# Two of a pair's four weight sums, from VectorE to a plain and an accumulating transfer

## The chip, the cores and the metric

The kernel runs on one core of a Trainium2 chip. The metric is the device time of one execution in microseconds (us). Of the kernel before, three timed runs and one profiled execution are given.

## The reference

A decoder layer on 512 tokens of width 1024, float32: a SwiGLU feed-forward, a mixer (dilated attention beside a gated linear recurrence), and a second SwiGLU feed-forward, each inside norms and a residual sum. The change lies in the two feed-forwards:

```
f = (silu(x @ w_gate) * (x @ w_up)) @ w_down      # 1024 -> 2816 -> 1024
h = h + 0.5 * rms_norm(f, norm_post)
```

## The kernel before, in words

**Number format.** A float32 product is made of three reduced ones. `split` (L301 to L303) makes a high part on ScalarE (L302) and a low part on VectorE (L303, the number less its high part); `mm3` and `seventh` multiply high by high, high by low and low by high.

**Feed-forward.** The 2816 hidden columns are 22 blocks of 128. The first 6 blocks (first feed-forward) or 3 (second) are multiplied plainly ("std"). Every later block f is a **pair**: its gate block g and its up block u, each 1024 x 128, are multiplied together by a Strassen-like scheme with 7 products in place of 8, with g and u as the two block columns. The rows of each are cut in two halves of 512 (g0, g1, u0, u1 in the tile: 4 row chunks of 128 columns side by side, so 128 x 512). The seven weight operands are g0, g1, u1 and four sums: u0+u1, u0+u1+g0, u0+g0 and u0+u1+g0+g1.

**`w_forms` (L684 to L702)** makes a pair's operands. It loads two raw tiles of 128 x 1024 (ur = u0 u1, gr = g0 g1) on the SP queue (L242; pool of 4 raw tiles), makes the four sums on VectorE (L691: u0+u1, L692: that + g0, L693: u0+g0, L696: the second + g1), and splits four tiles: a (g0, g1), b (the tile s12 with two sums), c (ur, one sum and u1) and d (the last sum). a, b and c are wide weight tiles (tag w8, 4 buffers), d is a narrow one (w4, 2 buffers). s12 has the tag s with 2 buffers. Products are named p1 to p7: a holds p1 and p2, b p6 and p5, c p7 and p4, d p3.

**`seven_on` (L733 to L760)** multiplies a pair from block 5 on in the order p1, p5, p6, p2, p7, p3, p4, 12 matmuls of 256 columns each (L729 to L731). The activation operand of p6 is the tile tx; the others' are tiles called big. ScalarE moves sums between PSUM tiles (L743), VectorE adds two results (L950, L955), and the result goes through `into` (L960 and L913 to L928) to become the operand of the down-projection.

**Down-projection.** It is made by seven products too, over groups of four blocks, in steps (`down7`, L1034 to L1052) that lie between the pairs of the next group: 12 or 24 matmuls of 512 columns (L1043 to L1045) and their weights by `d_forms` (L970 to L1002), which takes raw tiles and w8 tiles from the same pools.

**Order.** `ffn_order` (L66 to L90) writes the order of events: `prep` of pair f+1 (its `w_forms`) stands before `prod` of pair f. All of a pair's weight work is traced with a priority of 100 instructions ahead (AHEAD), moves out of PSUM with 200 (EVAC). A planner at compile time orders each engine's queue by these priorities and places the tiles; each engine then runs its queue strictly in order and waits for semaphores. Loads on SP follow one stream in device memory (`stream_plan`), in the order of their use, so a pair's two raw blocks lie one after the other there. The POOL queue issues transfers only: copies of activations (L655), the kept residual (L536, L1721, L1151) and gain rows (L449).

**The mixer** uses `w_forms` as well (through `pair_of`, L1340), for 16 pairs.

Of the kernel before, what the change touches and what calls it, by code (L numbers as in the profile page):

```python
# [10 lines left out]
F32 = mybir.dt.float32  # L11
F32R = mybir.dt.float32r
AF = mybir.ActivationFunctionType
ALU = mybir.AluOpType
AX = mybir.AxisListType

P = 128
T = 512
D = 1024
KC = D // P  # L20
NF = 22
FF_PARTS = ((0, 4), (4, 8), (8, 12), (12, 16), (16, 22))
NSTD = {1: 6, 2: 3}

SEVEN = range(4)
STEPS_AT = {1: ((6, 7, 7, 8), range(9, 13), range(13, 17), range(17, 21)),
# [5 lines left out]
RAW_W = 1024  # L32
# [3 lines left out]
AHEAD = 100  # L36
# [29 lines left out]
def ffn_order(n):  # L66

    order = [("std", f) for f in range(NSTD[n])]  # L70
    after = {}
    for a in SEVEN:
        for i, f in enumerate(STEPS_AT[n][a]):
            after.setdefault(f, []).append((a, i))
    ready = False
    for f in range(NSTD[n], NF):
        if not ready:
            order.append(("prep", f))
        steps = after.get(f, [])
        order += [("prepd",) + s for s in steps]  # L80
        ready = f + 1 < NF
        if ready:
            order.append(("prep", f + 1))
        order += [("seeds",) + s for s in steps[:1]]
        order.append(("prod", f))
        for m, s in enumerate(steps):
            if m:
                order.append(("seeds",) + s)
            order.append(("down7",) + s)
    return order  # L90
# [70 lines left out]
def stream_groups():  # L161

    groups, cur, w = [], [], 0
    for key, width in stream_plan():
        if w + width > RAW_W or (cur and cur[0][0][0] == "start"):
            groups.append(cur)
            cur, w = [], 0
        cur.append((key, w, width))
        w += width
    groups.append(cur)  # L170
    return groups
# [12 lines left out]
def hybrid_layer(ctx: ExitStack, tc: tile.TileContext, xT: bass.AP, xN: bass.AP, wst: bass.AP,  # L184
                 first: bass.AP, rows: bass.AP, consts: bass.AP, bias: bass.AP, out: bass.AP):
    nc = tc.nc
    DVE, ACT, PE = nc.vector, nc.scalar, nc.tensor
# [3 lines left out]
    wpool = ctx.enter_context(tc.tile_pool(name="wpool", bufs=4))  # L191
# [39 lines left out]
    groups = stream_groups()  # L231
    state = {"g": 0, "i": 0, "off": 0, "raw": None, "ahead": AHEAD, "split": None}
# [21 lines left out]
    def raw_two(key, dst=None):  # L254

        return [raw_of(key + (n,), None if dst is None else dst[:, i * RAW_W:(i + 1) * RAW_W])
                for i, n in enumerate(("lo", "hi"))]

    def fetch(key, slot=None, ahead=0):

        with tc.high_priority(offset=ahead if slot else state["ahead"]):
            src = raw_of(key)
            w = src.shape[-1]
            t = slot() if slot else w8() if w > 512 else w4()
            split(t[:, 0, :w], t[:, 1, :w], src)
            return t[:, 0, :w], t[:, 1, :w]

    def w8():
        return wpool.tile([P, 2, 1024], F32R, name="w8", tag="w8", bufs=4)

    def w4():
        return wpool.tile([P, 2, 512], F32R, name="w4", tag="w4", bufs=2)
# [28 lines left out]
    def split(dh, dl, src):  # L301
        state["split"] = ACT.activation(dh, src, AF.Copy).ins  # L302
        state["low"] = DVE.tensor_sub(dl, src, dh.bitcast(F32)).ins  # L303

    def acc_ps():
        return psum.tile([P, T], F32, name="acc", tag="acc", bufs=5)
# [23 lines left out]
    def gemm(ps, wt, x, sl=slice(0, T), ks=None):  # L330
        n = x.n
        a, b = k128(wt[0], n), k128(wt[1], n)
        for k in ks or range(n):
            mm3(ps, a[:, k, :], b[:, k, :], x.hi[k][:, sl], x.lo[k][:, sl], k == 0, k == n - 1)
# [346 lines left out]

    spool = [None]

    def w_forms(key):  # L684

        with tc.high_priority(offset=AHEAD):
            ur, gr = raw_two(key)
            u0, u1, g0, g1 = (r[:, i * 512:(i + 1) * 512] for r in (ur, gr) for i in range(2))
            s12 = spool[0].tile([P, 2, 512], F32, name="s12", tag="s", bufs=2)
            s1, s2 = s12[:, 0, :], s12[:, 1, :]  # L690
            DVE.tensor_add(s2, u0, u1)  # L691
            DVE.tensor_add(s1, s2, g0)  # L692
            DVE.tensor_add(u0, u0, g0)  # L693
            a, b, c, d = w8(), w8(), w8(), w4()
            split(a[:, 0, :], a[:, 1, :], gr)
            DVE.tensor_add(g1, s1, g1)  # L696
            split(b[:, 0, :], b[:, 1, :], s12.rearrange("p s c -> p (s c)"))
            split(c[:, 0, :], c[:, 1, :], ur)
            split(d[:, 0, :], d[:, 1, :], g1)
            lo, hi = slice(0, 512), slice(512, 1024)  # L700
            return {"p1": a[:, :, lo], "p2": a[:, :, hi], "p6": b[:, :, lo], "p5": b[:, :, hi],
                    "p7": c[:, :, lo], "p4": c[:, :, hi], "p3": d}  # L702
# [156 lines left out]
    def ffn(n, x, r, forms_x, apool, pss):  # L859
# [70 lines left out]
        def std_out(psg, psu, f):  # L930

            g = tmp("g")
            if r is None:
                ACT.activation(g, psg, AF.Silu)
                into(f, lambda dst, v: DVE.tensor_mul(dst, v(psu), v(g)))
                return
            u = tmp("u0")
            DVE.tensor_mul(g, psg, r)
            ACT.activation(g, g, AF.Silu)
            DVE.tensor_mul(u, psu, r)  # L940
            into(f, lambda dst, v: DVE.tensor_mul(dst, v(u), v(g)))
# [28 lines left out]
        def d_forms(a, i):  # L970

            x, w = sevens[a], {}

            def form(name, src):
                w[name] = w8()
                split(w[name][:, 0, :], w[name][:, 1, :], src)

            with tc.high_priority(offset=AHEAD):
                raw = [raw_of(("dq", n, a, q)) for q in SEVEN_RAW[i]]
                if i == 0:  # L980
                    x["sum"] = apool.tile([P, 2, D], F32, name="sum", tag="wd", bufs=1)[:, 0, :]
                sd = x["sum"]
                if i == 0:
                    g0, u0 = raw
                    form("p1", g0)
                    DVE.tensor_add(sd, g0, u0)
                    form("p7", sd)
                elif i == 1:
                    u1, = raw
                    form("p4", u1)  # L990
                    DVE.tensor_add(sd, sd, u1)
                    form("p6", sd)
                elif i == 2:
                    u0, u1 = raw
                    DVE.tensor_add(u0, u0, u1)
                    form("p5", u0)
                else:
                    g1, = raw
                    form("p2", g1)
                    DVE.tensor_add(sd, sd, g1)  # L1000
                    form("p3", sd)
            return w  # L1002
# [63 lines left out]

        keys = [(w, n, i) for i in range(NSTD[n]) for w in ("gate", "up")]
        forms = {}
        for ev in ffn_order(n):
            if ev[0] == "std":  # L1070
                j = ev[1]
                while len(pss) < 2 * j + 2:
                    pss.append(acc_ps())
                    gemm(pss[-1], fetch(keys[len(pss) - 1]), x)
                with tc.high_priority(offset=EVAC if j == NSTD[n] - 1 else 0):
                    std_out(pss[2 * j], pss[2 * j + 1], j)

                for step in steps[j:] if j == min(NSTD[n], 4) - 1 else steps[j:j + 1]:
                    step()
            elif ev[0] == "prep":  # L1080
                forms[ev[1]] = w_forms(("gu", n, ev[1]))
            elif ev[0] == "prepd":
                forms[ev[1:]] = d_forms(*ev[1:])
            elif ev[0] == "seeds":
                for g in groups(ev[2])[:3]:
                    seed(ev[1], *g)
            elif ev[0] == "down7":
                down7(*ev[1:], forms.pop(ev[1:]))
            else:
                prod(ev[1], forms.pop(ev[1]))  # L1090
        a = len(FF_PARTS) - 1
# [32 lines left out]
    for k in range(KC):  # L1124
        wh, wl, raw = wts[k]
# [77 lines left out]
    with ExitStack() as mx:  # L1203
# [126 lines left out]
        order = [("pair",) + p for ps in pairs for p in ps] + [("pair", 52 + c, 53 + c) for c in range(0, KC, 2)]  # L1330
        forms = {}
# [8 lines left out]
        def pair_of(key):  # L1340

            i = order.index(key)
            if i + 1 < len(order):
                forms[order[i + 1]] = w_forms(order[i + 1])
            return forms.pop(key)

        def qk(hd):
# [147 lines left out]
        for c in range(0, KC, 2):  # L1495
            g, u = tmp("g"), tmp("u")
            seven_wide(t, pair_of(("pair", 52 + c, 53 + c)), [g[:, h] for h in HALVES], [u[:, h] for h in HALVES],
                       then=gate)
# [10 lines left out]
    with ExitStack() as mx:  # L1509
# [183 lines left out]
        for c in range(KC):  # L1693
            if c < 3:
                ps = pss[c]
            else:
# [17 lines left out]
                 {(1, 3): lambda: (bd2.turn(0), bd2.turn(1))})  # L1714
    keys = [(w, 2, i) for i in range(NSTD[2]) for w in ("gate", "up")]
    pss = gemm_first(keys[:NFIRST], u2, [spare(ap2)["tx"]],
# [5 lines left out]
    grow5, _ = gains(ap2, 4)  # L1722
# [138 lines left out]
```

## Time and profile before

| | |
|---|---|
| Three timed runs | 1209.67, 1210.02, 1210.19 us |
| Profiled execution | 1209.61 us, of which the span of the instructions is 1207.8 |
| First feed-forward's pairs | about 60 to 310 us |
| Second feed-forward's pairs | about 880 to 1168 us |
| Bytes moved | 149.77 MB, 124 GB/s over the span |
| SP queue's share of the 16 DMA engines | 32.9% |
| POOL queue's share of the 16 DMA engines | 4.3% |

How to read it: engines are PE (TensorE matmul), PEld (its weight loads), DVE (VectorE), ACT (ScalarE), POOL (GpSimd) and SP (SyncE, which only issues transfers). In a row of groups stand line, engine, operation, written tile <- read tiles, shapes, count, then busy us in all, mean ns of one, and the idle time of the engine just before, with what ended most of it. In a row of the timeline stand start and duration in us, then what runs, and in brackets idle time before it and what ended it. A row of DMA issues gives count, size of one, and the median time from issue to landing. Ends of matmuls are modelled and overlap the next one's start, so the pace of matmuls is read from their starts.

### The profile page before, as it was taken

What the parts mean: (1) busy time and instruction counts of PE and PEld (TensorE: products, weight loads), DVE (VectorE), ACT (ScalarE), POOL (GpSimd) and SP (SyncE); (2) the same over time, 40 slices, a digit from 0 to 9 for tenths busy, and PEclk for the clock granted to TensorE, in tenths of its full rate; (3) what the DMA queues carried; (4) which work ended last, traced back from release to release, by engine and by line L of the source; (5) the groups of instructions that cost most, each with busy time, mean ns of one, the idle gap of its engine ahead of it and who ended that gap; (6) DMA issues with size and microseconds to landing.
All of it is one profiled execution on the core that took longest, in us unless ns stands there. A gap on an engine that the chain in (4) does not pass through costs nothing.

```text
span 1207.8 us, 18850 instructions
## 1 busy us (share of the span) xinstructions
PE 1198.6 (99%) x7222; PEld 1070.1 (89%) x7222; DVE 1033.3 (86%) x1626; ACT 831.8 (69%) x1447; POOL 26.1 (2%) x51
## 2 busy tenths in 40 slices
PE   9999999999999999999999999999999999999997
PEld 8889999999888888888888888888899999999996
DVE  7999888989689899999868999774799888889964
ACT  6566787887566576777736988734566687778763
POOL 0000000000011000000000000000100000000000
PEclk9999999999999999999999999999999999999999
DMA  7224343434725232222323532235443333333441
GB/s 267 88 92 139 120 139 109 137 117 150 250 106 154 71 101 91 89 87 80 122 67 110 176 121 88 88 107 189 140 142 121 121 125 117 128 120 126 125 173 70
DMA packets 45819, 149.77 MB, mean 124 GB/s; under 512 B 5152, under 2 KB 8608, under 8 KB 45728
## 3 DMA queue, kind: packets, MB, share of 16 engines
q1 hardware_dynamic: 38160, 131.09, 32.9%
q0 software_dynamic: 7280, 17.30, 4.3%
q8 instruction: 56, 0.92, 0.3%
q14 instruction: 35, 0.29, 0.1%
q10 hardware_dynamic: 288, 0.17, 0.0%
HBM read 138.06 MB, written 6.29 MB: 120 GB/s over the span
## 4 chain that ended last, share of the span: by engine, by line
PE 92%; DVE 4%; DMA 2%; ACT 1%; issue 1%; DVEq 0%; ACTq 0%
PE acc L779 10%; PE acc L729 9%; PE acc L731 9%; PE acc L730 9%; PE acc L315 7%; PE acc L317 7%; PE acc L316 7%; PE acc L780 5%; PE aux L1043 4%; PE aux L1044 4%; PE aux L1045 4%; PE acc L433 2%; PE acc L432 2%; PE acc L431 2%; DVE w L303 2%; DMA raw<-in_w 2%
## 5 line engine op out<-in xcount | busy, mean ns | idle before, releaser
L303 DVE TENSOR_TENSOR w<-raw,w 128x1024 fp32r<-128x1024 f32 (+1 forms) x272 | 296.9, 1097 | 32.2 <-ACT w L302 31.4
L302 ACT ACTIVATE w<-raw 128x1024 fp32r<-128x1024 f32 (+1 forms) x272 | 259.5, 958 | 90.0 <-PE acc L317 48.2
L729 PE MATMUL acc<-big,w 128*128 128x256 f32 x860 | 243.6, 283 | 0.0
L731 PE MATMUL acc<-big,w 128*128 128x256 f32 x860 | 243.4, 283 | 0.0
L730 PE MATMUL acc<-big,w 128*128 128x256 f32 x860 | 243.3, 283 | 0.0
L729 PEld LDWEIGHTS acc<-big,w 128*128 128x128 f32 x860 | 164.8, 192 | 1.8
L730 PEld LDWEIGHTS acc<-big,w 128*128 128x128 f32 x860 | 164.8, 192 | 1.5
L731 PEld LDWEIGHTS acc<-big,w 128*128 128x128 f32 x860 | 164.8, 192 | 0.0
L779 PE MATMUL acc<-big,w 128*128 128x512 f32 x380 | 136.5, 398 | 0.0
L780 PE MATMUL acc<-big,w 128*128 128x256 f32 x380 | 107.5, 283 | 0.0
L1043 PE MATMUL aux<-w,xf 128*128 128x512 f32 x224 | 87.3, 392 | 0.6 <-ACT w L302 0.6
L1044 PE MATMUL aux<-w,xf 128*128 128x512 f32 x224 | 87.5, 391 | 0.0
L1045 PE MATMUL aux<-w,xf 128*128 128x512 f32 x224 | 87.2, 389 | 0.0
L779 PEld LDWEIGHTS acc<-big,w 128*128 128x128 f32 x380 | 71.4, 188 | 16.0 <-ACT acc L784 0.2
L780 PEld LDWEIGHTS acc<-big,w 128*128 128x128 f32 x380 | 71.7, 189 | 0.3
L303 DVE TENSOR_TENSOR w<-s,w 128x1024 fp32r<-128x1024 f32 x51 | 62.2, 1220 | 3.2 <-ACT w L302 2.7
L315 PE MATMUL acc<-xf,w 128*128 128x512 f32 (+1 forms) x168 | 59.2, 354 | 0.0
L316 PE MATMUL acc<-xf,w 128*128 128x512 f32 (+1 forms) x168 | 58.7, 350 | 0.0
L317 PE MATMUL acc<-xf,w 128*128 128x512 f32 (+1 forms) x168 | 58.5, 349 | 0.0
L302 ACT ACTIVATE w<-s 128x1024 fp32r<-128x1024 f32 x51 | 53.9, 1057 | 6.2 <-PE acc L731 3.0
L779 PE MATMUL acc<-rb,w 128*128 128x512 f32 x152 | 55.5, 397 | 0.0
L743 ACT ACTIVATE c<-acc 128x256 f32<-128x256 f32 x68 | 25.8, 383 | 35.3 <-PE acc L731 35.3
(458 smaller groups left out, 2919.5 us busy)
## 6 DMA issues: line engine op xcount, KB each, us to landing
raw<-in_w SPq DMA_DIRECT2D x232, 512.0 KB, 3.5
big<-xf POOLq DMA_DIRECT2D x6, 512.0 KB, 3.3
gains<-in_rows POOLq DMA_DIRECT2D x5, 512.0 KB, 5.4
h<-in_x SPq DMA_DIRECT2D x8, 256.0 KB, 5.1
h<-in_xn POOLq DMA_DIRECT2D x4, 512.0 KB, 6.7
kept_m<-h POOLq DMA_DIRECT2D x4, 512.0 KB, 2.9
vals<-in_w SPq DMA_DIRECT2D x4, 512.0 KB, 6.0
h<-kept_m POOLq DMA_DIRECT2D x4, 512.0 KB, 6.2
```

Source lines behind the costliest of these rows:

```text
L302: state["split"] = ACT.activation(dh, src, AF.Copy).ins
L303: state["low"] = DVE.tensor_sub(dl, src, dh.bitcast(F32)).ins
L315: PE.matmul(ps, wh, xh, start=first, stop=False)
L316: PE.matmul(ps, wh, xl, start=False, stop=False)
L317: PE.matmul(ps, wl, xh, start=False, stop=last)
L729: PE.matmul(ps, wh, xh, start=start and k == 0, stop=False, skip_group_check=True)
L730: PE.matmul(ps, wh, xl, start=False, stop=False, skip_group_check=True)
L731: PE.matmul(ps, wl, xh, start=False, stop=k == 3, skip_group_check=True)
L779: PE.matmul(part, wh, at(BOTH, k), start=start and k == 0, stop=False, skip_group_check=True)
L780: PE.matmul(cross, wl, at(0, k), start=False, stop=k == 3, skip_group_check=True)
L1043: PE.matmul(ps, xh, wh, start=first and j == 0, stop=False, skip_group_check=True)
L1044: PE.matmul(ps, xh, wl, start=False, stop=False, skip_group_check=True)
```

## The change

For the pairs from block 8 on in the first feed-forward and from block 5 on in the second, two sums are made by transfers that POOL issues. `sums_ahead` takes a tile s, fills both halves with u0 by a plain transfer, and adds u1 to the first half and g0 to the second by an accumulating transfer, which waits until the plain one has landed. It is traced right after the operands of the pair before have been made, that is ahead of the `prod` of the pair two before. `w_forms_summed` then loads g0 and g1 (one transfer) and u1 (a transfer of half the size) on SP, and makes the other two sums on VectorE: u0+u1+g0 into the empty half of ur, and that + g1 into the second half of gr. Splits are a (g0, g1: p1, p2), b (s: p5, p7), c (ur: p6, p4) and d (p3). In the mixer nothing changes: 16 pairs never reach the index 99.

```
@@ -21,6 +21,7 @@
 NF = 22
 FF_PARTS = ((0, 4), (4, 8), (8, 12), (12, 16), (16, 22))
 NSTD = {1: 6, 2: 3}
+SUMMED = {1: 8, 2: 5}
 
 SEVEN = range(4)
 STEPS_AT = {1: ((6, 7, 7, 8), range(9, 13), range(13, 17), range(17, 21)),
@@ -681,7 +682,56 @@
 
     spool = [None]
 
-    def w_forms(key):
+    starts, summed, end = {}, {}, 0
+    for grp in groups[1:]:
+        starts[grp[0][0]] = end
+        end += (grp[-1][1] + grp[-1][2]) * P
+
+    def rows_of(key, o, *dims):
+        return bass.AP(tensor=wst.tensor, offset=wst.offset + starts[key + ("lo",)] + o,
+                       ap=[[RAW_W, P], *dims, [1, T]])
+
+    def sums_ahead(key):
+
+        with tc.high_priority(offset=AHEAD):
+            s = spool[0].tile([P, 2, T], F32, name="s12", tag="s", bufs=2)
+            nc.gpsimd.dma_start(s, rows_of(key, 0, [0, 2]))
+            nc.gpsimd.dma_start(s, rows_of(key, T, [P * RAW_W - T, 2]), accum_op=ALU.add)
+            summed[key] = s
+
+    def w_forms_summed(key):
+
+        s = summed.pop(key)
+        with tc.high_priority(offset=AHEAD):
+            g = state["g"]
+            assert state["i"] == 0 and [k for k, _, _ in groups[g] + groups[g + 1]] == [key + ("lo",), key + ("hi",)]
+            assert state["off"] == starts[key + ("lo",)]
+            gr, ur = (wpool.tile([P, RAW_W], F32, name="raw", tag="raw", bufs=4) for _ in range(2))
+            nc.sync.dma_start(gr, rows_of(key, P * RAW_W, [T, 2]))
+            nc.sync.dma_start(ur[:, T:], rows_of(key, T))
+            state["g"], state["off"] = g + 2, state["off"] + 2 * P * RAW_W
+            a, b, c, d = w8(), w8(), w8(), w4()
+            split(a[:, 0, :], a[:, 1, :], gr)
+            DVE.tensor_add(ur[:, :T], s[:, 0, :], gr[:, :T])
+            split(b[:, 0, :], b[:, 1, :], s.rearrange("p s c -> p (s c)"))
+            split(c[:, 0, :], c[:, 1, :], ur)
+            DVE.tensor_add(gr[:, T:], ur[:, :T], gr[:, T:])
+            split(d[:, 0, :], d[:, 1, :], gr[:, T:])
+            lo, hi = slice(0, T), slice(T, D)
+            return {"p1": a[:, :, lo], "p2": a[:, :, hi], "p5": b[:, :, lo], "p7": b[:, :, hi],
+                    "p6": c[:, :, lo], "p4": c[:, :, hi], "p3": d}
+
+    def w_forms(key, then=None):
+
+        if key in summed:
+            w = w_forms_summed(key)
+        else:
+            w = w_forms_made(key)
+        if then:
+            sums_ahead(then)
+        return w
+
+    def w_forms_made(key):
 
         with tc.high_priority(offset=AHEAD):
             ur, gr = raw_two(key)
@@ -1078,7 +1128,8 @@
                 for step in steps[j:] if j == min(NSTD[n], 4) - 1 else steps[j:j + 1]:
                     step()
             elif ev[0] == "prep":
-                forms[ev[1]] = w_forms(("gu", n, ev[1]))
+                f = ev[1]
+                forms[f] = w_forms(("gu", n, f), ("gu", n, f + 1) if SUMMED[n] <= f + 1 < NF else None)
             elif ev[0] == "prepd":
                 forms[ev[1:]] = d_forms(*ev[1:])
             elif ev[0] == "seeds":
@@ -1341,7 +1392,7 @@
 
             i = order.index(key)
             if i + 1 < len(order):
-                forms[order[i + 1]] = w_forms(order[i + 1])
+                forms[order[i + 1]] = w_forms(order[i + 1], order[i + 2] if 99 <= i + 2 < len(order) else None)
             return forms.pop(key)
 
         def qk(hd):
```

## The prediction

> **What bounds the kernel now.** I read the page's busy line first, then the table by stretches, then what TensorE waits for, and last the timeline around one of those waits.
>
> ```profile
> span 1207.8 us, 18850 instructions
> PE 1198.6 (99%) x7222; PEld 1070.1 (89%) x7222; DVE 1033.3 (86%) x1626; ACT 831.8 (69%) x1447; POOL 26.1 (2%) x51
> ```
>
> TensorE (PE) is busy for all but 9.2 us of the span. VectorE (DVE), which the change relieves, has 86%. The execution took 1209.61 us, 1.8 beyond its span, and the median of the three timed runs is 1210.02, so one execution stands within 0.4 us of it.
>
> ```profile
> 240.00:260.00 20.00, 20.00 (x145) 18.92 (x145) 18.35 (x23) 17.34 (x31) 0.00 (x0) 1.00 0.33 105
> 300.00:320.00 20.00, 20.00 (x129) 18.27 (x128) 13.64 (x18) 11.79 (x20) 2.09 (x4) 1.00 0.85 304
> 1000.00:1020.00 20.00, 19.80 (x153) 19.02 (x152) 14.88 (x20) 14.56 (x26) 0.00 (x0) 1.00 0.42 142
> 1020.00:1040.00 20.00, 20.00 (x143) 18.80 (x142) 19.97 (x28) 16.37 (x28) 0.00 (x0) 1.00 0.31 106
> ```
>
> Columns after the stretch: its length, busy us of PE, PEld, DVE, ACT and POOL, the granted clock, the DMA share, GB/s. In the first feed-forward PE has no idle time. In the second it loses 0.20 us in a stretch where DVE has 5 us to spare, and none in the next, where DVE is busy for 19.97 of 20. So a full DVE doesn't by itself stop PE. At 300 to 320 the DMA engines are busy for 0.85 of the time and PE still works for 20.00.
>
> ```profile
> PE aux L1043 <- ACT w L302: 0.6, 3, 0.2
> PE aux L1378 <- DVE qk L792: 0.7, 1, 0.7
> PE acc L729 <- ACT acc L743: 0.4, 1, 0.4
> ...
> 1013.28 1.05 ACT L302 ACTIVATE w<-raw 128x1024 fp32r<-128x1024 f32 x1
> 1013.90 0.28 PE L731 MATMUL acc<-big,w 128*128 128x256 f32 x1
> 1014.39 0.73 PE L1043 MATMUL aux<-w,xf 128*128 128x512 f32 x2 [0.20 <-ACT w L302]
> ```
>
> Only the first wait lies in the stages that change (the other two come at the attention and before the recurrence). Matmuls overlap, so the loss is read from starts: 256-column products start 0.12 us apart, here 0.49 passed, 0.37 is lost. Three times that is **1.1 us, about all that PE can get back in the feed-forwards**. What ends it is the high part of a down-projection weight on ACT, not a sum on DVE.
>
> **The change, part by part.** Pairs 8 to 21 of the first feed-forward (14) and 5 to 21 of the second (17) change: 31.
>
> *Removed.*
>
> ```profile
> L692 DVE TENSOR_TENSOR s<-s,raw 128x512 f32<-128x512 f32 x51 | 34.9, 685 | 12.3 <-DMA raw<-in_w 12.1
> L691 DVE TENSOR_TENSOR s<-raw 128x512 f32<-128x512 f32 x51 | 34.9, 684 | 6.1 <-DMA raw<-in_w 6.0
> L693 DVE TENSOR_TENSOR raw<-raw 128x512 f32<-128x512 f32 x51 | 34.8, 682 | 0.0
> ```
>
> The transfers make u0+u1 (L691) and u0+g0 (L693). The sums of L692 and L696 stay on DVE. That is 31 x (0.684 + 0.682) = 42 us of DVE's 1033. DVE's waits for raw weights in front of the sums (up to 18 us over 51 pairs) shrink too. All of it lies beside PE, which lost 1.1 us there. Value: 0; ends: 0 and -1.1.
>
> *Added: two transfers from POOL for each pair.*
>
> ```profile
> raw<-in_w SPq DMA_DIRECT2D x232, 512.0 KB, 3.5
> big<-xf POOLq DMA_DIRECT2D x6, 512.0 KB, 3.3
> h<-in_xn POOLq DMA_DIRECT2D x4, 512.0 KB, 6.7
> ...
> 860.46 0.76 POOL L655 DMA_DIRECT2D big<-xf  x1 [6.27 <-ACT xf L553]
> ```
>
> The plain one moves u0 twice (512 KB), the accumulating one 512 KB of u1 and g0. Issue: 0.76 us on POOL each. Landing of the plain one: 3.3, at most 6.7. No row shows an accumulating transfer: at the low end it costs a plain one, 3.3; at the high end it makes three passes (source, old sum, new sum) at the slowest row, 20.1; I take two passes at the nearest row of that size, 6.6. It can't gain anything. The chain plain, landing, accumulate, landing is 0.76 + 3.3 + 0.76 + 6.6 = **11.4 us**, between 8.1 and 28.3.
>
> What covers it:
>
> ```profile
> 1100.75 1.22 DVE L303 TENSOR_TENSOR w<-s,w 128x1024 fp32r<-128x1024 f32 x1
> 1127.89 1.22 DVE L303 TENSOR_TENSOR w<-s,w 128x1024 fp32r<-128x1024 f32 x1
> 1154.67 1.22 DVE L303 TENSOR_TENSOR w<-s,w 128x1024 fp32r<-128x1024 f32 x1 [0.53 <-ACT w L302]
> ...
> 292.18 1.19 POOL L449 DMA_DIRECT2D gains<-in_rows  x2 [291.73 <-DVE w L303]
> 1140.58 0.54 POOL L449 DMA_DIRECT2D gains<-in_rows  x1 [257.70 <-DVE w L303]
> ```
>
> The sum tile has two buffers, so a pair's transfer can begin when the split of the pair two before it has read its sums. The three rows are such splits, each two pairs after the other, where pairs follow fastest: from the end of one, 1101.97, to the high part on ACT ahead of the next (1.06 us before 1127.89) are 24.9 us; the second interval gives 24.5. So 11.4 fits with 13 to spare; only the upper end, 28.3, doesn't. POOL does nothing before 292 us in the first feed-forward and between 882.88 and 1140.58 in the second: nothing is queued ahead of the new transfers. The gains behind them wait for the last down-projection sum anyway. If the cover were gone, what is queued behind the waiting sum on DVE is the low part of the next split and then the PSUM sums L955, L950 and L960, for which the next products wait. Value: 0.
>
> *Loads on SP.* The pair's gate block comes first (512 KB) and of the up block only its second half (256 KB), still on two of the four raw buffers. Bytes moved go from 1.0 to 1.75 MB a pair, 24 MB more in all. No PE time goes with a higher DMA share as such (300 to 320, above), but a load beside POOL's traffic lands later:
>
> ```profile
> raw<-in_w SPq DMA_DIRECT2D x12, 512.0 KB, 4.7
> ```
>
> This is the same load in the stretch 290 to 330, with six 512 KB transfers of POOL: 4.7 instead of 3.5, **1.2 us later**. The Trainium skill, "DMA: Bandwidth & Descriptors", section "Issuing engines are not separate DMA queues", speaks against the change: transfers from any engine end on the same 16 DMA engines and interleave, so a second issuer brings no bandwidth. The trace agrees, by those 1.2 us; by that rule the rival below grows, and my sum stays.
>
> *Moved: which weights share a buffer.* Split b now holds p5 and p7 (was p6 and p5), c holds p6 and p4 (was p7 and p4). Products run p1, p5, p6, p2, p7, p3, p4, 12 matmuls x 0.12 = 1.44 us each. The four wide weight buffers are handed on as products end:
>
> ```profile
> 1003.96 0.28 PE L731 MATMUL acc<-tx,w 128*128 128x256 f32 x1
> 1004.56 1.05 ACT L302 ACTIVATE w<-raw 128x1024 fp32r<-128x1024 f32 x1
> 1005.40 0.28 PE L731 MATMUL acc<-big,w 128*128 128x256 f32 x1
> 1005.72 1.06 ACT L302 ACTIVATE w<-s 128x1024 fp32r<-128x1024 f32 x1
> 1009.72 0.28 PE L731 MATMUL acc<-big,w 128*128 128x256 f32 x1
> 1010.50 1.04 ACT L302 ACTIVATE w<-raw 128x1024 fp32r<-128x1024 f32 x1
> ...
> 1027.84 1.22 DVE L303 TENSOR_TENSOR w<-raw,w 128x1024 fp32r<-128x1024 f32 x1
> 1031.47 0.28 PE L729 MATMUL acc<-tx,w 128*128 128x256 f32 x1
> 1059.85 1.22 DVE L303 TENSOR_TENSOR w<-raw,w 128x1024 fp32r<-128x1024 f32 x1
> 1062.73 0.28 PE L729 MATMUL acc<-tx,w 128*128 128x256 f32 x1
> ```
>
> p6 alone reads the tile tx, which dates the products. The next pair's a follows the end of p6, b the end of p2, c the end of p4: ACT makes them as buffers come free. With b held until p7, a and b come 1.44 us later each; c as before. But c is now needed at p6, not 2 x 1.44 = 2.88 us later at p7. Its low part ends at 1029.06 and at 1061.07, p6 starts at 1031.47 and 1062.73: **2.4 and 1.66 us remain** where 5.3 and 4.5 were. Value: 0, as long as c isn't more than 1.66 us later than today.
>
> The sum: 1209.61 + 0 + 0 + 0 = 1209.6 against the profiled execution; against the median of the runs, **1210.0**. Most of the 42 us of DVE time turns into DVE's idle time.
>
> **Rivals.**
>
> *Late c (slower).* Place: the c split, read by p6. a and b come 1.44 us later into the stretch where DVE also makes the PSUM sums; if DVE hands all of it on and the up half lands 1.2 us later, c is 2.64 late: 0.24 over the margin of 2.4, 0.98 over that of 1.66. A mean of 0.6 on half of the 31 pairs is 9 us, 1219; on all of them 19 us, 1229. It decides from 1.66 us on. For: the loads lengthen, and the margin shrinks by 2.88 in every pair. Against: DVE gets 1.37 us back per pair, about what the move takes.
>
> *Late sums (slower).* The accumulating transfer is near its upper end, 28.3 against 24.5: 3.8 us of waiting in the about 8 pairs that follow fastest, 30 us, 1240. Then the sums aren't ahead of their use at all, and the change doesn't do what it says. Against: 13 us of slack at my value.
>
> *Faster.* PE gets back the 1.1 us of its waits in the feed-forwards, and the planner, whose order of every queue is made anew, happens also to lose those of the mixer (0.7 and 0.4 in the list): about 1207.3. The first alone, 1208.9, can't be told from no change. Against: the 1.1 us end on ACT and on a buffer that PE frees.
>
> **How the numbers follow.** About 0.2% (2.4 us) is what a measurement of this kernel tells from no change. Forecast, within 1208.3 to 1212.4: 0.62. Late c: 0.26. Late sums: 0.06. Faster: 0.06. So faster 0.06, same 0.62, slower 0.32. The range runs from 1208.3, which leaves out the faster case, to 1218, which takes in the forecast and the lighter half of late c; what is left out is some 0.2. The forecast's own range is 1208.3 to 1212.4.
>
> **What the profile of the changed kernel would show.** The four groups of sums of pairs fall from 51 to 20 instructions each, two new ones of 31 appear, DVE's busy time falls by about 42 us, PE's matmul count stays, and PE's idle time stays near 9 us. The accumulating transfer's landing should be 3.3 to 20.1, nearest 6.6, and no engine should wait for long on the sum tile. Late c shows as PE waits in front of products on tx, ended by ACT or DVE w of lines 302 and 303; late sums as DVE or ACT waits ended by a DMA into s. I am wrong if PE's waits in the feed-forwards grow to more than 2.4 us, or if a wait that I read as a buffer's was DVE's and PE gains more than 2.4.

## The result, and the profile after

The changed kernel takes 1252.59 us (median of 4 runs, 1248.14 to 1255.90) against 1210.11 of the kernel before in the same comparison (4 runs, 1209.67 to 1210.26): ratio **1.035, 95% interval 1.0315 to 1.0384, slower**. The profiled execution took 1253.95 us, 1.75 beyond its span. The prediction said 1210.0 with a range to 1218.0: it was wrong, by 42.6 us. Against the kernel before of the same comparison the change loses 42.5 us.

The page of the kernel after, its span and its busy line:

```profile
span 1252.2 us, 18905 instructions
PE 1216.0 (97%) x7222; PEld 1080.3 (86%) x7222; DVE 998.3 (80%) x1564; ACT 833.9 (67%) x1447; POOL 86.8 (7%) x113
```

DVE's busy time fell by 35.0 us (1033.3 before), where the prediction had 42, mostly because it added up the durations of 62 sums, while on DVE the end of one overlaps the start of the next (L692 of 0.69 us and L693 start 0.60 apart, at 1001.07 and 1001.67 of before). PE now has 36.2 us without work in the span (9.2 before), and for the same 7222 matmuls it is busy 17.4 us longer. These are two separate losses: PE waits, and PE at times runs slower. Most of the waits have one shape. The kernel after, its waits (engine, tile and line, what ended the wait: us in all, times, longest):

```profile
PE aux L1093 <- ACT aux L1082: 15.3, 7, 3.1
PE acc L779 <- ACT c L886: 4.5, 1, 4.5
PE aux L1093 <- ACT facc L1098: 3.6, 2, 2.3
...
DVE raw L1045 <- DMA raw<-in_w: 45.8, 8, 7.8
DVE raw L715 <- DMA s<-in_w: 12.7, 2, 6.7
```

L1093 is the first product of a down-projection step (L1043 before), L1082 the ScalarE copy that seeds its PSUM tile. Neither is touched by the change. L1045 is the sum of the step i = 2, `DVE.tensor_add(u0, u0, u1)` (L995 before). DVE waits 45.8 us there for a raw weight, at 8 places, the 4 groups of both feed-forwards. In the kernel before, the same operation waited 0.9 us over two places:

```profile
DVE raw L995 <- DMA raw<-in_w: 0.9, 2, 0.6
```

**One such place, step by step.** The kernel after, the timeline from 1069 to 1091 us: POOL's transfers, SP's loads, then DVE, ACT and PE.

```profile
1069.99 0.75 POOL L698 DMA_DIRECT2D s<-in_w  x1 [9.28 <-DVE w L304]
1075.14 1.20 POOL L699 DMA_DIRECT2D s<-in_w  x1 [4.40 <-DMA s<-in_w]
1073.26 2.68 SPq L243 DMA_DIRECT2D raw<-in_w  x2
1074.36 1.23 DVE L304 TENSOR_TENSOR w<-raw,w 128x1024 fp32r<-128x1024 f32 x1 [0.52 <-ACT w L303]
1083.04 1.22 DVE L1045 TENSOR_TENSOR raw<-raw 128x1024 f32<-128x1024 f32 x1 [7.45 <-DMA raw<-in_w]
1085.32 0.42 DVE L1005 TENSOR_TENSOR u<-acc,c 128x256 f32<-128x256 f32 x1
1085.65 0.41 DVE L1000 TENSOR_TENSOR g<-acc,c 128x256 f32<-128x256 f32 x1
1086.10 0.42 ACT L1001 ACTIVATE g<-g 128x256 f32<-128x256 f32 x1 [5.03 <-DVE g L1000]
1089.09 0.59 ACT L1082 ACTIVATE aux<-ea 128x512 f32<-128x512 f32 x1
1089.73 0.80 PE L1093 MATMUL aux<-w,xf 128*128 128x512 f32 x1 [2.84 <-ACT aux L1082]
```

The second of the two loads at 1073.26 is issued at 1075.61 (its own record in the trace), 0.47 us after the accumulating transfer, and lands at 1082.91: **7.30 us**. DVE has nothing else that its strict order allows, waits 7.45 us and makes the sum at 1083.04. Behind that sum in DVE's queue stand the PSUM sums u (L1005) and g (L1000). For g waits ACT's silu (L1001, idle for 5.03 us), and behind the silu in ACT's queue stands the seed of L1082, which starts 3.0 us after it. PE needs it and stands 2.84 us.

The same place in the kernel before, the timeline around 1051:

```profile
1046.74 1.22 DVE L303 TENSOR_TENSOR w<-raw,w 128x1024 fp32r<-128x1024 f32 x1
1050.19 1.22 DVE L303 TENSOR_TENSOR w<-sum,w 128x1024 fp32r<-128x1024 f32 x1 [1.63 <-ACT w L302]
1051.72 1.23 DVE L995 TENSOR_TENSOR raw<-raw 128x1024 f32<-128x1024 f32 x1 [0.30 <-DMA raw<-in_w]
1052.86 0.42 DVE L955 TENSOR_TENSOR u<-acc,c 128x256 f32<-128x256 f32 x1
1054.33 0.42 DVE L950 TENSOR_TENSOR g<-acc,c 128x256 f32<-128x256 f32 x1
```

There the load was issued at 1047.99 and landed at 1051.59, after 3.60 us. From the issue to the start of g it is 6.3 us before and 10.0 after: the 3.7 us by which the landing is longer arrive at ACT undiminished. Read the 0.30: before the change, this load already landed after DVE had become free (1051.41). At all eight places it landed between 0.4 us before and 0.5 us after that moment. Nothing covered a delay.

**Half of the wait is another delay: the load also starts later.** Each load waits for one of the four raw buffers. Before, a split (1046.74, to 1047.96) frees it, and from the load's issue it takes DVE 3.4 us until it is ready for the sum: the sum L693 at 1047.88, which the change removes, a wait, and the split at 1050.19, which after the change stands behind L1045 (1084.18). After, the buffer is freed by the split that stands right ahead of the sum (1074.36, to 1075.58): DVE is ready as the load is issued, and the whole landing is its wait. Over the eight places, the issue came 3.4 to 4.1 us ahead of DVE before; after, 3.4 ahead at the first, 1.3 at the next two, and with DVE ready at the other five. The landing took 3.4 to 4.5 us before and 4.5 to 8.0 after. Summed over the places, DVE's wait grew by about 23 us from the lost head start and 22 from the longer landing. At one place where the landing stayed short (4.5 us, a wait of 3.3), PE lost only 0.6 us (at 221.80), so a part of each wait is absorbed behind DVE.

The fourth step's sum (L1050) waits for its load too, 6.4 us at four places; behind the longest, 2.74 us at 101.07, PE starts 2.5 us late.

**The second kind of place** are the two waits of DVE on the sum tile itself (12.7 us), at the first and the last summed pair of the second feed-forward. The kernel after, the timeline there:

```profile
905.82 1.22 DVE L304 TENSOR_TENSOR w<-s,w 128x1024 fp32r<-128x1024 f32 x1
916.66 1.21 DVE L304 TENSOR_TENSOR big<-ts,big 128x1024 fp32r<-128x1024 f32 x1
918.19 0.71 POOL L698 DMA_DIRECT2D s<-in_w  x1 [18.84 <-DVE big L304]
922.94 1.22 POOL L699 DMA_DIRECT2D s<-in_w  x1 [0.72 <-DMA s<-in_w]
933.10 0.69 DVE L715 TENSOR_TENSOR raw<-s,raw 128x512 f32<-128x512 f32 x1 [5.96 <-DMA s<-in_w]
...
1166.85 1.22 DVE L304 TENSOR_TENSOR w<-s,w 128x1024 fp32r<-128x1024 f32 x1
1168.48 0.75 POOL L698 DMA_DIRECT2D s<-in_w  x1 [7.05 <-DVE w L304]
1173.07 1.20 POOL L699 DMA_DIRECT2D s<-in_w  x1 [3.83 <-DMA s<-in_w]
1182.43 0.69 DVE L715 TENSOR_TENSOR raw<-s,raw 128x512 f32<-128x512 f32 x1 [6.75 <-DMA s<-in_w]
```

The chain takes 14.9 us at the first (918.19 to 933.07, when it lands) and 13.9 at the last. The reader that comes first is the sum of L715, and DVE was ready for it 9.0 and 7.2 us after the chain's begin. PE then starts 4.7 and 3.1 us late.

**PE at half speed.** The kernel after, the table by stretches (length, busy us of PE, PEld, DVE, ACT, POOL, granted clock, DMA share, GB/s):

```profile
935.00:940.00 5.00, 3.89 (x18) 3.90 (x19) 4.98 (x9) 2.94 (x6) 0.00 (x0) 0.52 0.64 105
...
1085.00:1090.00 5.00, 2.16 (x9) 1.26 (x8) 5.00 (x9) 3.81 (x7) 0.32 (x1) 0.88 0.34 105
1090.00:1095.00 5.00, 5.00 (x18) 4.42 (x19) 3.87 (x6) 3.66 (x6) 1.13 (x2) 0.50 0.67 193
```

After the wait the granted clock is 0.50, with PE busy for all of the 5 us and 18 matmuls done. The pace of starts says the same: products of 256 columns start 0.21 us apart until 1095.45, then 0.12 again.

From the starts of all matmuls in the feed-forwards I divide what each kernel loses against the median distance of each shape: distances over 0.25 us too long (waits), those of the halved clock (0.21 us for 256 columns, 0.43 for 512: slow clock), the rest. Us, from each kernel's trace:

| kernel | waits | slow clock | rest |
|---|---|---|---|
| before | 1.1 | 0 | 0.8 |
| after | 32.4 | 11.4 | 3.5 |

The difference, 45.4, is about that of the spans (44.4). Little or nothing was lost elsewhere.

### The profile page after: what moved, and what is told of

It reads as the page before. It is cut to its first block, busy times and chain, and to the rows that moved or that the text cites. A ratio compares the mean times of both kernels' runs of the same rounds, so it can differ in the third digit from the quotient of the medians.

```text
span 1252.2 us, 18905 instructions
## 1 busy us (share of the span) xinstructions
PE 1216.0 (97%) x7222; PEld 1080.3 (86%) x7222; DVE 998.3 (80%) x1564; ACT 833.9 (67%) x1447; POOL 86.8 (7%) x113
## 4 chain that ended last, share of the span: by engine, by line
PE 75%; DVE 9%; DMA 7%; ACT 6%; issue 3%; POOL 0%; DVEq 0%; POOLq 0%; ACTq 0%
PE acc L829 9%; PE acc L316 6%; PE acc L318 6%; PE acc L317 6%; PE acc L779 6%; PE acc L781 6%; PE acc L780 6%; DMA raw<-in_w 5%; PE acc L830 5%; DVE w L304 4%; ACT w L303 3%; PE aux L1093 2%; DMA s<-in_w 2%; PE aux L1095 2%; PE aux L1094 2%
## 5 line engine op out<-in xcount | busy, mean ns | idle before, releaser
L779 PE MATMUL acc<-big,w 128*128 128x256 f32 x860 | 247.1, 287 | 4.5 <-ACT c L886 4.5
L780 PE MATMUL acc<-big,w 128*128 128x256 f32 x860 | 246.7, 287 | 0.0
L781 PE MATMUL acc<-big,w 128*128 128x256 f32 x860 | 246.6, 287 | 0.0
L779 PEld LDWEIGHTS acc<-big,w 128*128 128x128 f32 x860 | 168.8, 196 | 6.7 <-ACT c L886 4.7
L780 PEld LDWEIGHTS acc<-big,w 128*128 128x128 f32 x860 | 168.4, 196 | 2.0
L781 PEld LDWEIGHTS acc<-big,w 128*128 128x128 f32 x860 | 168.3, 196 | 0.0
L1093 PE MATMUL aux<-w,xf 128*128 128x512 f32 x224 | 90.1, 407 | 21.6 <-ACT aux L1082 15.3
L830 PE MATMUL acc<-big,w 128*128 128x256 f32 x380 | 107.5, 283 | 0.0
L1094 PE MATMUL aux<-w,xf 128*128 128x512 f32 x224 | 89.9, 401 | 1.3 <-DVE w L304 1.3
L1095 PE MATMUL aux<-w,xf 128*128 128x512 f32 x224 | 89.6, 400 | 0.0
L829 PEld LDWEIGHTS acc<-big,w 128*128 128x128 f32 x380 | 71.3, 188 | 15.8 <-ACT acc L834 0.2
L1093 PEld LDWEIGHTS aux<-w,xf 128*128 128x128 f32 x224 | 42.5, 192 | 34.4 <-ACT aux L1082 18.3
L830 PEld LDWEIGHTS acc<-big,w 128*128 128x128 f32 x380 | 71.7, 189 | 0.3
```

Source lines behind the costliest of these rows:

```text
L779: PE.matmul(ps, wh, xh, start=start and k == 0, stop=False, skip_group_check=True)
L780: PE.matmul(ps, wh, xl, start=False, stop=False, skip_group_check=True)
L781: PE.matmul(ps, wl, xh, start=False, stop=k == 3, skip_group_check=True)
L829: PE.matmul(part, wh, at(BOTH, k), start=start and k == 0, stop=False, skip_group_check=True)
L830: PE.matmul(cross, wl, at(0, k), start=False, stop=k == 3, skip_group_check=True)
L1093: PE.matmul(ps, xh, wh, start=first and j == 0, stop=False, skip_group_check=True)
```

## The experiments

**Theories.** A: the transfers from POOL, the accumulating one most, crowd SP's loads of raw weights, and the third down-projection step's sum, whose load has no cover, comes late. B: the rearranged operands and load order do it (c needed earlier, the prediction's first rival). C: any second transfer from POOL of that size does it, accumulating or not. None of the three names the lost head start, and no run takes it apart from the longer landing. Medians, ratios to the kernel before in the same comparison, and the division of above. The division is that of one traced run, which for e2k_both is its fastest (1237.38). Runs of the change lie between 1248.14 and 1255.90, so differences to its median are good to a few us:

| kernel | us | ratio (95%) | waits | slow clock | rest |
|---|---|---|---|---|---|
| e1_plain | 1233.80 | 1.0204 (1.0182 to 1.0226) | 20.3 | 1.3 | 2.9 |
| e2_onchip | 1212.64 | 1.0026 (1.0015 to 1.0036) | 4.0 | 0 | 1.6 |
| e2k_both | 1242.44 | 1.0274 (1.0239 to 1.0310) | 23.3 | 4.0 | 3.5 |
| e4_spare | 1220.91 | 1.0093 (1.0076 to 1.0110) | 10.1 | 3.3 | 1.0 |
| e5_inner | 1211.81 | 1.0016 (1.0007 to 1.0025) | 3.0 | 0 | 0.9 |
| e6_half | 1245.01 | 1.0290 (1.0271 to 1.0308) | 29.0 | 4.1 | 3.8 |
| e7_before_spare | 1209.99 | 1.0003 (0.9994 to 1.0012) | 1.1 | 0 | 1.0 |
| e8_ends | 1242.31 | 1.0266 (1.0240 to 1.0291) | 26.6 | 8.5 | 3.1 |
| e9_late | 1221.54 | 1.0094 (1.0081 to 1.0107) | 10.4 | 0 | 3.2 |

### e1_plain: the second transfer doesn't accumulate

```
-            nc.gpsimd.dma_start(s, rows_of(key, T, [P * RAW_W - T, 2]), accum_op=ALU.add)
+            nc.gpsimd.dma_start(s, rows_of(key, T, [P * RAW_W - T, 2]))
```

> The changed kernel with its second transfer plain instead of accumulating (it overwrites the sum tile, so two weight sums are wrong; same bytes, same queue, same waits). Theory A (the accumulating transfer crowds the raw weight loads, 7.8 us to land, loads beside it 5 to 8): loads beside the second transfer land in 4 to 5 us, the wait of the down-projection sum L1045 falls from 5.7-7.8 us to 2-4, time 1212 to 1228. Rival B (the new sharing of weight buffers and load order): no change, 1245 to 1256. Rival C (any transfer of that size from POOL crowds the loads alike): 1240 to 1256.

Measured: 1233.8, 18.8 less than the change. The two kernels' second transfers, L699, first accumulating (after), then plain (e1_plain), each with the issue's duration on POOL (ns, min/median/max) and the landing:

```profile
L699 POOL DMA_DIRECT2D s<-in_w x31: 1182/1207/1228, 75.0 to 1173.1; - x31
DMA to landing us min/median/max: 5.7/7.8/10.1
```

```profile
L699 POOL DMA_DIRECT2D s<-in_w x31: 724/724/737, 74.9 to 1156.4; - x31
DMA to landing us min/median/max: 4.1/5.7/7.7
```

The plain one lands 2.1 us sooner and is issued 0.48 sooner. But the loads still come late. The waits of e1_plain:

```profile
PE aux L1093 <- ACT aux L1082: 10.2, 7, 2.6
...
DVE raw L1045 <- DMA raw<-in_w: 41.0, 8, 7.0
```

Neither A in its strong form nor C holds: a plain transfer keeps more than half of the loss, the accumulation adds the rest, of which the slow clock is 10.1 us (11.4 to 1.3): its clock falls once, after its longest wait (2.79 us, at 1074.89).

### e2_onchip and e2k_both: the rearrangement without and with the transfers

e2_onchip keeps the new operands and the order of loads, but loads both halves of u and makes all four sums on DVE; e2k_both is the same with the two transfers into s besides, whose result DVE then writes over.

```
-            nc.gpsimd.dma_start(s, rows_of(key, 0, [0, 2]))
-            nc.gpsimd.dma_start(s, rows_of(key, T, [P * RAW_W - T, 2]), accum_op=ALU.add)
...
-            nc.sync.dma_start(ur[:, T:], rows_of(key, T))
+            nc.sync.dma_start(ur, rows_of(key, 0, [T, 2]))
...
+            DVE.tensor_add(s[:, 0, :], ur[:, :T], ur[:, T:])
+            DVE.tensor_add(s[:, 1, :], ur[:, :T], gr[:, :T])
```

> The changed kernel's operands, products and load order (gate block first), but no transfers: all four sums on VectorE. Theory A: 1209 to 1214, PE's waits in the feed-forwards under 3 us. Rival B: 1235 to 1256, with waits in front of products on tx.

> As e2_onchip, with the two transfers added into the same sum tile, whose values VectorE then overwrites with its own sums: against e2_onchip only the transfers differ. Theory A: 1240 to 1262, L1045 waiting 5 us or more at most of its 8 places, as in the changed kernel. Rival B: the same as e2_onchip within 5 us.

Measured: 1212.64 and 1242.44. The rearrangement costs about 3 us; the transfers, on top of it, 29.8 (1242.44 - 1212.64), though nothing reads what they bring. B is not the cause. A part of the 29.8 is not crowding: at the first summed pair of the second feed-forward DVE has to wait 4.8 us for the transfers before it may write over s, and PE starts 4.3 us late behind that. The waits of e2_onchip show the sum of L1045 nearly on time:

```profile
DVE raw L1045 <- DMA raw<-in_w: 6.6, 6, 2.1
```

In e2k_both, A's time came out but not its place. The third step's sum waits 11.9 us at its eight places (at most 2.6, where A asked for 5 or more), since its loads are issued 3.1 to 5.6 us ahead of DVE there. The late loads show at the pair's own sums, ahead of which DVE now waits for raw weights at 21 pairs (12 pairs and 12.9 us in e2_onchip). Its waits:

```profile
DVE s L715 <- DMA raw<-in_w: 32.6, 21, 3.3
```

### e4_spare: the uncovered load doesn't wait for a buffer

The tile "sum" of the down-projection is 128 x 2 x 1024, of which half is unused. The u1 of step i = 2 goes there, so its load needs no raw buffer and can begin long before the accumulating transfer; u0 gets the raw buffer that comes free earlier. The transfers are all kept.

```
-                raw = [raw_of(("dq", n, a, q)) for q in SEVEN_RAW[i]]
+                raw = [raw_of(("dq", n, a, q), x["spare"] if (i, q) == (2, "u1") else None) for q in SEVEN_RAW[i]]
                 if i == 0:
-                    x["sum"] = apool.tile([P, 2, D], F32, name="sum", tag="wd", bufs=1)[:, 0, :]
+                    both = apool.tile([P, 2, D], F32, name="sum", tag="wd", bufs=1)
+                    x["sum"], x["spare"] = both[:, 0, :], both[:, 1, :]
```

> The changed kernel, with the second raw block of down-projection step 3 (u1, read by L1045) loaded into an unused half of the tile that holds that part's sum, so that its load needn't wait for a raw buffer (2.35 us in one cycle) and is on its way before the accumulating transfer begins. Theory A: the wait of L1045 falls by 2 to 5 us at 7 places, time 1222 to 1240. Rival B: 1248 to 1256.

Measured: 1220.91, just below A's range. **31.7 of the 42.5 us go** with this one edit. It undoes both halves of the wait. From the second place on, u0's load, now the later one, is issued 2.1 to 3.7 us ahead of DVE and lands after 3.7 to 4.7 us, though the same transfers run. So the 31.7 price the late load, not the crowding alone. What is left stands in the waits of e4_spare: the late sums at the two ends.

```profile
PE acc L779 <- ACT c L886: 3.9, 1, 3.9
PE aux L1094 <- ACT aux L1083: 2.3, 1, 2.3
...
DVE raw L715 <- DMA s<-in_w: 10.6, 2, 5.3
DVE raw L1046 <- DMA raw<-in_w: 7.2, 5, 2.3
```

### e7_before_spare: the same edit without the transfers

> The kernel before, without any transfers from POOL, with the one edit that brought the change from 1252.6 to 1220.9: the third down-projection step's u1 goes into the unused half of the sum tile and so needs no raw buffer. If that edit only takes the transfers' collision away, it brings nothing here, where loads land in 3.5 us: 1208.5 to 1210.5. If it is a gain of its own, of which the change only showed the size, it is faster by more: below 1207.

Measured: 1209.99, ratio 1.0003 (0.9994 to 1.0012). The edit has no gain of its own; in e4_spare it only undid what the change had done to these loads, their late start and their longer landing.

### e5_inner and e8_ends: without the first and the last summed pair

Both leave pair 21 to DVE in each feed-forward, and pair 5 in the second (28 summed pairs in place of 31). e5_inner has the spare half too, e8_ends hasn't.

```
-SUMMED = {1: 8, 2: 5}
+SUMMED = {1: 8, 2: 6}
...
-                forms[f] = w_forms(("gu", n, f), ("gu", n, f + 1) if SUMMED[n] <= f + 1 < NF else None)
+                forms[f] = w_forms(("gu", n, f), ("gu", n, f + 1) if SUMMED[n] <= f + 1 < NF - 1 else None)
```

> The spare-half kernel, with two more edits: the second feed-forward's summed pairs begin at 6 in place of 5, and pair 21 isn't summed by transfers in either feed-forward (28 pairs in place of 31). If what is left of the loss there (1220.9 against 1209.7) is the two waits of DVE on the sum tile at the first and the last summed pair of the second feed-forward (TensorE stood 3.9 and 2.3 us behind them, and its clock then fell for about 3 us), both go: 1211 to 1215. If the loss is spread over all summed pairs, three pairs fewer of 31 take a tenth of it: 1219 to 1221. If the first summed pair is late wherever it stands, the wait moves to pair 6: about 1217.

> The change with only the two edits at the ends: the second feed-forward's summed pairs begin at 6 in place of 5, and pair 21 isn't summed by transfers in either feed-forward; no spare half. If the loss of 42.6 is two parts that add up, the late load of the down-projection's third step (31.7, taken away by the spare half alone) and the late sums at the ends (9.1 more, taken away on top of it), this leaves the first: 1240 to 1245. If the two hang together, so that either edit does most of the work, it is below 1230; if the ends only mattered once the loads were on time, about 1250.

Measured: e5_inner 1211.81, e8_ends 1242.31. Alone, the ends give 10.3 (1252.59 - 1242.31) and the spare half 31.7; together they give 40.8. So, as far as runs that spread over 8 to 12 us tell, the loss is two parts that add up. e5_inner is the telling kernel, for 28 of the 31 chains still run in it. Its busy line, then its second transfer and the pair's gate load beside it:

```profile
PE 1199.2 (99%) x7222; PEld 1070.2 (88%) x7222; DVE 1002.9 (83%) x1570; ACT 831.9 (69%) x1447; POOL 80.9 (7%) x107
```

```profile
L699 POOL DMA_DIRECT2D s<-in_w x28: 1196/1212/1228, 74.6 to 1123.7; - x28
DMA to landing us min/median/max: 6.5/7.8/9.9
...
L710 SPq DMA_DIRECT2D raw<-in_w x28: 327/328/328, 86.5 to 1124.7; - x28
DMA to landing us min/median/max: 4.4/5.1/8.0
```

The accumulating transfers are as long as in the change (7.8), and the pairs' gate loads longer still (5.1 in median, up to 8.0; 4.7 in the change, where the raw loads of before took 3.5). It costs next to nothing there, because these loads have slack: the pairs' first sum on DVE waits for a raw load at 2 of 28 pairs, 1.9 us in all. And the 30 us of busy time taken from DVE (1002.9 against 1033.3) bring nothing visible: 0.16% slower (0.07 to 0.25), at the edge of what can be told.

### e6_half: half of the accumulation

```
-            nc.gpsimd.dma_start(s, rows_of(key, T, [P * RAW_W - T, 2]), accum_op=ALU.add)
+            nc.gpsimd.dma_start(s[:, 0, :], rows_of(key, T), accum_op=ALU.add)
...
+            DVE.tensor_add(s[:, 1, :], s[:, 1, :], gr[:, :T])
```

> The change with half of the accumulating transfer: only u0+u1 is accumulated (256 KB), u0+g0 is finished on VectorE from the plain copy of u0 (31 sums of 0.68 us come back). If the accumulating transfer crowds the raw loads in proportion to what it moves, the loss lies between that of the change (42.6) and what the plain transfer alone would leave: the landing of the accumulating one about 5, the wait ahead of the down-projection's sum shorter, 1222 to 1240. If any second transfer from POOL costs the same whatever its size, 1245 to 1255. If the extra sum on VectorE matters, above 1240 with DVE, not a DMA, ahead of TensorE's waits.

Measured: 1245.01, above the range in proportion and at the lower edge of the next one; but ahead of TensorE's waits stand ScalarE's seeds, as in the change. The waits of e6_half:

```profile
DVE raw L1046 <- DMA raw<-in_w: 37.4, 8, 6.5
DVE s L715 <- DMA raw<-in_w: 17.6, 5, 4.2
```

The 256 KB accumulating transfer lands after 5.5 us (7.8 for 512 KB), the late load costs DVE 37.4 in place of 45.8, but the sum that came back to DVE (L715 of this kernel) waits for the gate load, 17.6 us at 5 pairs, a wait that the change hasn't. So the kernel changes two things, and the loss by size can't be read from it.

### e9_late: the same sum made late without transfers

```
                     u0, u1 = raw
+                    for _ in range(3 + a):
+                        DVE.tensor_max(u1, u1, u1)
                     DVE.tensor_add(u0, u0, u1)
```

> The kernel before, no transfers from POOL. Ahead of the third down-projection step's sum, VectorE is given 3, 4, 5 and 6 extra operations on the loaded tile (each takes the larger of a number and itself, 1.22 us each by the row of that shape, so 3.7, 4.9, 6.1 and 7.3 us) at the four groups of each feed-forward. If the change lost its time because that sum came late, whatever made it late, the same stalls appear without any transfer: TensorE loses nothing to 1 us at 3.7, about 3 at 7.3, waits at the down-projection's products behind ScalarE's seed (line 1032 and after), and its clock falls after the longer ones: 1218 to 1230, nearest 1225. If the lateness of that sum alone is harmless and it is the traffic itself that slows the engines, it stays within 1213.

Measured: 1221.54. The time lies in the range, but not by the reason given, and the run doesn't tell the theories apart. The waits of e9_late have no product behind a seed at the head:

```profile
PE aux L1045 <- ACT w L302: 2.3, 5, 0.5
PE acc L729 <- DVE u L960: 2.3, 2, 1.1
```

The planner laid the extra operations out over 12 us (five of them from 1059.05 to 1071.04 in the timeline of the third group of the second feed-forward) with other work between them, u and g among it. So that sum may stand 13.5 us behind the first of them (1072.58) without a product waiting behind a seed: what costs in the change is what stands behind the wait in DVE's queue. I read it so that the plan spreads a lateness that it counts, while a load's falls on one instruction; no run tests that. It does show the other side: 38.9 us more busy time on DVE (1072.2) cost 11.7 here, where 30 us less bring nothing (e5_inner).

## Why the prediction was wrong, step by step

**The step that failed** is "Loads on SP". It saw that a load beside POOL's traffic lands later, "1.2 us later", said that no PE time goes with a higher DMA share as such, and gave the loads no term in the sum, without naming work that hides a late load. Three things were off. The size: beside the accumulating transfer the load took 3.7 us longer at the place shown (7.30 against 3.60). The 1.2 was a difference of medians, beside plain transfers; at the eight places the load took 4.5 to 8.0 us, where it had taken 3.4 to 4.5. The start: the step says that the pair's blocks are "still on two of the four raw buffers" and doesn't ask when these come free. At the third down-projection step they came free up to 4.1 us later against DVE's queue, and that makes as much of DVE's wait as the longer landing. And the cover, which decides: that step's load had none, as 1051.72 [0.30 <-DMA] of the kernel before says. The prediction looked for who waits for the pair's loads, and not for the other loads on the same queue and the same four buffers. e4_spare prices the late load at 31.7 us. How much of it is crowding and how much the late start stays open: a kernel with the two sums gone from DVE and no transfers beside the loads was not run. e2k_both against e2_onchip shows that the transfers alone cost up to 29.8 us in a kernel where the head start is kept.

**The chain's cover** failed at the two ends. The chain itself was sized fairly: 11.4 estimated, 13.9 to 14.9 at the ends and 14.7 at the place above; the accumulating landing 7.8, within 3.3 to 20.1 and near the 6.6 taken; its issue 1.2 in place of 0.76. The cover of 24.5 was measured to ScalarE's split of s. But the first reader of s in the changed kernel is DVE's sum L715, which can stand ahead of that split: 7.2 us after the chain's begin at the last pair, 9.0 at the first. At the first pair the chain began only at 918.19, 11 us after the split of the pair two before (905.82 to 907.04). What released it is the split of the tile ts (916.66 to 917.87): ts, a difference of activations (L667, L668), is taken from the same pool under the same tag s, so it holds one of the two buffers that the prediction counted as free for the sums of weights. Together: 9.1 to 10.3 us (e5_inner against e4_spare, e8_ends against the change). This is the "late sums" rival at two places, not at its condition of 28.3 us.

**The clock** was in no step: 11.4 us of the traced run's loss.

**Late c** (0.26) was the wrong rival: e2_onchip, which has its moved operands, is 1.8 to 4.4 us slower (1.0015 to 1.0036 of 1209.7), where the rival asked for 9 to 19. It lacks the later loads that the rival also asked for; but in the change itself no wait of PE at a pair's products is ended by a split of weights.

**DVE's relief is worth 0** held as far as the runs show: e5_inner, with the sums of 28 pairs gone from DVE, got nothing back, though it carries what the transfers cost. The bound, 1.1 us in the feed-forwards, was not reached.

**The rule of the Trainium skill** ("DMA: Bandwidth & Descriptors", section "Issuing engines are not separate DMA queues") that transfers of all issuers end on the same 16 DMA engines was weighed rightly as speaking against the change, and then given to the wrong rival (c), because the loads whose lateness decides weren't looked for.

The sign to look for was named: PE's waits in the feed-forwards over 2.4 us (they are 32.4).

## What to carry to other kernels

Before adding transfers beside a tuned stream of loads, list every load that shares its queue, its buffers or its moment, and find for each the instruction that waits for it in the trace of before: a wait of 0.3 us that a DMA ends is a load without cover, and its delay goes on to whatever stands behind that wait in the strict queues, less what is absorbed on the way. Look also at which instruction frees the load's buffer, and how far ahead of the reader it stands: where work between the two is taken out or moved, the load's head start goes with it. A mean landing, and a mean DMA share, hide this; one load in eight places made 31.7 of 42.5 us. Give such a load a buffer of its own, so that it can begin sooner: that, with the three end pairs left out, made nearly the same traffic almost free (e5_inner), though it couldn't make a relief of DVE worth anything where PE was already full.

## What the runs showed of the hardware

**The clock falls after short waits.** In the six kernels with longer waits (after, e1_plain, e2k_both, e4_spare, e6_half, e8_ends), matmul starts in the feed-forwards came 2.3 to 4.7 us too late 21 times, and 18 times the next ones came at half the pace, at a cost of 1.2 to 2.5 us each. Just below that it goes both ways: after 2.21 and 1.97 us (e2k_both) the clock fell, after 2.15 (e8_ends), 2.01 (e1_plain) and 1.96 (e6_half) it didn't; below these it never fell. That it isn't the length alone shows in e6_half too, its table by stretches: after a start that is 2.94 us late (1034.98) the clock stays at 1.00, after one that is 2.57 late (1081.47) it falls.

```profile
1035.00:1040.00 5.00, 5.00 (x40) 4.91 (x41) 1.19 (x1) 1.46 (x4) 0.86 (x1) 1.00 0.97 314
...
1083.00:1088.00 5.00, 5.00 (x34) 4.71 (x33) 4.21 (x6) 4.27 (x9) 0.85 (x1) 0.80 0.84 259
```

The shortest wait with a fall, in e2k_both (idle for 1.81 us, 1.97 late by the starts), its timeline and its table by stretches:

```profile
1161.08 0.38 PE L781 MATMUL acc<-tx,w 128*128 128x256 f32 x1 [1.81 <-ACT acc L795]
...
1162.00:1167.00 5.00, 5.00 (x32) 5.00 (x31) 3.56 (x7) 2.16 (x4) 1.06 (x1) 0.66 0.95 285
```

A clock of 0.66 over these 5 us is 3.4 us at half. By the clock's records in the six traces, the 20 falls in the feed-forwards last 3.41 us (14 times) or 6.83 us (6 times).

The Trainium skill, "TensorE: Matmul & The Clock Gate", section "Part 1: The HAM clock gate", has the clock at half after an idle window of about 3.4 us, with a window that runs freely. The half agrees (0.50); the length doesn't, since falls came after waits of 2.84 us (above) and less. A free window would fit with waits of one length ending either way, but no run here varied where in the window a wait falls. The price of a PE wait thus has a step: from about 2 us on, 1.2 to 2.5 us can come on top.

**An accumulating transfer** of 512 KB holds POOL's issue for 1.2 us (a plain one of the same shape 0.72) and lands 2.1 us later than the plain one, in median. What goes on inside it isn't shown.
